# The first two feature-block pairs of w13 as whole blocks, with the sums of x taken meanwhile

## The chip, the cores and the metric

The kernel runs on one core of one Trainium2 chip. Five engines work side by side, each in its own order: TensorE (PE in the rows; PEld is its weight load), VectorE (DVE), ScalarE (ACT), GpSimd (POOL) and SyncE (SP), whose queue issues the weight loads. The metric is device time of one execution in microseconds. The kernel before took 2494.87 us, the median of three runs (2494.54 to 2494.98).

## The reference, cut to what matters

The program is a two-layer encoder with 512 tokens and a model width of 1024. Each layer has a SwiGLU feed-forward block, three token mixers side by side, and a second feed-forward block. The change touches only the first product of the feed-forward blocks, which runs four times (two blocks in each of two layers):

```python
def swiglu(h, w13, w2):
    a, g = jnp.split(h @ w13, 2, axis=-1)
    return (jax.nn.silu(a) * g) @ w2

x = x + 0.5 * swiglu(rms_norm(x, ffn1_norm[l]), ffn1_w13[l], ffn1_w2[l])
```

`w13` has 1024 rows and 2 x 2816 columns: 22 feature blocks of 128 for the value half `a` and 22 for the gate half `g`. All is float32.

## The kernel before

**Layout.** x is kept transposed, as 8 tiles of 128 features by 512 tokens. Each float32 operand of a product is split into a high part in fp32r and a low part (what the high part leaves), and each product is three matmuls: high by high, high by low, low by high. The split of a tile is one cast on ScalarE (the high part) and one subtraction on VectorE (the low part). Weights arrive from SyncE's queue in chunks of 128 x 1024 (`wraw`) and are split in the same way (`whi`, `wlo`, L77 and L78). Raw, split and summed chunks share a pool of 15 slots, so a load waits until a slot is free.

**w13 by seven products instead of eight.** The rms norm's division by the root mean square is put off until after the product, so x only needs its gain. The kernel takes the 8 x tiles in 4 pairs (an even and an odd tile) and cuts the 512 tokens into a left and a right half. For value and gate halves this makes a 2 x 2 by 2 x 2 product, which `wide` (L462) does with seven half-width products instead of eight, at the price of sums on both sides. On the x side, `even` (L413) and `odd` (L424) make the sums `T1` to `T4` from each pair of tiles, and split them. On the weight side, `products` (L91) adds chunks (`wsum`, L104) and yields split chunks in order, three ahead of their use. The 22 feature blocks of each half go in 11 groups, `d` = 0 to 10, of two value blocks and their two gate blocks. One product is a call of `step` (L451): 24 matmuls of 256 columns. So one group is 7 x 24 = 168 matmuls and a stage 11 x 168 = 1848. Four chunks are loaded for each group, four `wsum` are made, and seven chunks are split.

The products of a group share PSUM banks: `11`, `T2`, `T3` and `T4` go one after another into one bank, which ScalarE copies out in between (`copy`, L490); `21` has a bank of its own; `T1` and `22` share a third. The next `T` product into a bank can't start before the copy is out. `gated` multiplies by the norm (`R`) and takes the Silu.

**The norm.** GpSimd squares each x tile and adds it up (`square_sum`, L322): 16 operations, the last of which ends after the last x tile is there. TensorE then transposes the sum (`st`), VectorE reduces it, GpSimd takes the power (`r`), TensorE spreads it (`pr`), ScalarE copies it out as `R` (L350).

**Order.** The tile framework's scheduler sets the order on each engine from its own cost estimates when the program is built; in the first feed-forward block the x side's instructions on ScalarE, VectorE and GpSimd are kept in the order in which the code has them (`manual_schedule`). Each engine takes its instructions strictly in that order. In the first feed-forward block of layer 0 the x tiles come by DMA; in the other three stages they come from the stage before (`pw`, the mixer's output product, or `po`, the product with w2), tile by tile, and VectorE adds each to x (L1049 or L562).

**After w13.** `ffn` (L546) splits the 22 products (`a`, L309) and multiplies by w2 with `mm3` (L218 to L220, 512 columns): the first four output tiles with the feature blocks as the outer loop, so the first matmuls need the first `a`.

Of the kernel before, what the change touches and what calls it, by code (L numbers as in the profile page):

```python
# [12 lines left out]
ALU = mybir.AluOpType  # L13
# [26 lines left out]
class Stream:  # L40
# [23 lines left out]
    def _split(self, upto):  # L64
        while self.ready < min(upto, self.k.nch) and not self.summed(self.ready):
            c = self.ready
            self.load(c + self.k.AHEAD)
            self.split[c] = self.parts(self.raw.pop(c))
            self.ready += 1
# [21 lines left out]
    def products(self, l, name, n):  # L91
# [15 lines left out]
        def start(d):  # L107
            h = held[d] = {"11": raw(d, 0, 0)}
            return self.parts(h["11"], self.cuts(self.pos // CH - 1))

        yield start(0)
        yield start(1)
        for d in range(n):
# [8 lines left out]
            yield self.parts(h["12"])  # L122
# [3 lines left out]
            if 0 < d < n - 1:  # L126
# [27 lines left out]
class Kernel:  # L154
# [95 lines left out]
    def group_rstd(self, pss, srcs, xs, at=(4, 6)):  # L250

        res = g = None
        for k, _ in enumerate(self.group(pss, srcs, xs), 1):
# [159 lines left out]
    def even(self, j, gcol):  # L413

        H = T // 2
        t0, b12 = self.u(name="f0"), self.u(name="fb")
        self.nc.scalar.activation(t0[:, 0:H], self.x[j][:, 0:H], AF.Copy, scale=gcol)
        self.nc.scalar.activation(b12[:, 0:H], self.x[j][:, H:T], AF.Copy, scale=gcol)
        self.nc.vector.tensor_tensor(t0[:, H:T], t0[:, 0:H], b12[:, 0:H], ALU.subtract)
        f0 = self.split(t0, "f0")  # L420
        self.forms.append({"11": [t[:, 0:H] for t in f0], "T1": [t[:, H:T] for t in f0]})
        self.half = t0, b12

    def odd(self, j, gcol):  # L424
# [3 lines left out]
        t0, b12 = self.half  # L428
        f = self.forms[-1]
        t1, t2, t3 = self.u(name="f1"), self.u(name="f2"), self.u(name="f3")  # L430
        nc.scalar.activation(t1, self.x[j], AF.Copy, scale=gcol)
        nc.vector.scalar_tensor_tensor(t2[:, H:T], t0[:, H:T], -1.0, t1[:, H:T], ALU.mult, ALU.subtract)
        nc.vector.tensor_tensor(t2[:, 0:H], t1[:, H:T], b12[:, 0:H], ALU.subtract)
        nc.vector.scalar_tensor_tensor(t3[:, 0:H], t2[:, H:T], -1.0, t1[:, 0:H], ALU.mult, ALU.subtract)
        f1, f2 = self.split(t1, "f1"), self.split(t2, "f2")
        p = j // 2
        if p % 2 == 0:
            self.f3 = self.pair("f3")
        c = slice(p % 2 * H, p % 2 * H + H)
        f3 = self.split_to(t3[:, 0:H], [t[:, c] for t in self.f3])  # L440
        f["21"], f["22"] = [t[:, 0:H] for t in f1], [t[:, H:T] for t in f1]
        f["T3"], f["T2"] = [t[:, 0:H] for t in f2], [t[:, H:T] for t in f2]
        f["T4"] = f3

    def next_form(self, j, gcol):
        (self.odd if j % 2 else self.even)(j, gcol)
        if j == 0:
            self.sqacc = self.u(name="sqacc")
        self.square_sum(self.sqacc, self.x[j], j == 0)
# [12 lines left out]
    def wide(self, l, name):  # L462
# [20 lines left out]
        g = self.rstd(self.sqacc, D, self.att)  # L483
        out, b1, s1 = [], {}, {}
        v = lambda t: t.rearrange("p (e c) -> p e c", e=2)
        state = {}
# [10 lines left out]

        def gated(b, s, half):
            t = self.u(name="t")
            nc.vector.tensor_tensor(t, b, s, ALU.add)  # L500
            nc.vector.tensor_tensor(v(t), v(t), state["R"][:, None, half * H:half * H + H].broadcast_to([P, 2, H]), ALU.mult)
# [3 lines left out]
        start(0)  # L505
        start(1)
        for d in range(n):
            a = [self.u(name="a") for _ in range(2)]
            b2, b3 = self.acc("b"), self.att("b")
            if d == 0:  # L510
                w6, w2, w5 = w(), w(), w()
                for pairs in (range(3), range(3, 4)):
                    self.step(b1[d], w6, "T2", False, pairs)
                    self.step(b2, w2, "21", True, pairs)
# [646 lines left out]
```

## Time and profile before

| what | us |
|---|---|
| median of 3 runs | 2494.87 |
| profiled execution | 2494.28 |
| its span, first to last instruction | 2492.5 |
| w13 of layer 0, first block | to 263.69 from the start of the program |
| w13 of layer 0, second block | 896.87 to 1132.12 |
| w13 of layer 1, first block | 1252.91 to 1485.17 |
| w13 of layer 1, second block | 2118.76 to 2354.00 |

The stages are read from TensorE's rows in order of time: from the first matmul of L459 of a stage to the first matmul into `po`. All other times in this document are us from the start of the span of the profiled execution, unless a row gives ns. "L459" is the matmul of `step`.

### The profile page before, as it was taken

To read this page: it belongs to the slowest core of one execution; us is meant where nothing else is said; L and a number is where in the kernel's file an instruction comes from. 1 tells how busy PE (TensorE), PEld (TensorE's weight loads), DVE (VectorE), ACT (ScalarE), POOL (GpSimd) and SP (SyncE) were. 2 spreads that over 40 slices of the span, in tenths; PEclk is the share of its full clock that TensorE was granted. 3 is DMA by queue.
4 is the path that set the end of the run, shared out by engine and by line. 5 is a ranking of instruction groups with operands and counts; after the bars stand their busy time and mean duration, and the time that the engine had idled before them with its cause. 6 is when DMAs were issued, how large, how long until landed. Compare 5 with 4: busy or idle time off the path is not lost. (4 is left out here: it accounts for less than half of the span.)

```text
span 2492.5 us, 35789 instructions
## 1 busy us (share of the span) xinstructions
PE 2413.5 (97%) x14592; PEld 2146.9 (86%) x14592; DVE 1793.4 (72%) x2575; ACT 1154.5 (46%) x1774; POOL 291.4 (12%) x232
## 2 busy tenths in 40 slices
PE   5999999999999989999999999999999999899997
PEld 4999888888888879998889998888888888899986
DVE  7888655766677698885598884466667777888843
ACT  4444422455555544444255453234655664544520
POOL 3000023100001230000210001230000014100011
PEclk9999999999999999999999999999999999999998
DMA  3333433112121313333223332311221222233331
GB/s 112 102 102 102 127 93 115 51 60 82 63 75 61 119 60 104 109 104 119 92 77 102 104 125 93 112 62 52 76 77 60 68 93 94 77 107 107 120 100 43
DMA packets 62661, 224.22 MB, mean 90 GB/s; under 512 B 7216, under 2 KB 7360, under 8 KB 62496
## 3 DMA queue, kind: packets, MB, share of 16 engines
q1 hardware_dynamic: 61056, 218.19, 27.8%
q8 instruction: 114, 1.87, 0.3%
q0 software_dynamic: 864, 2.70, 0.3%
q10 hardware_dynamic: 576, 1.05, 0.1%
q14 instruction: 51, 0.42, 0.1%
HBM read 219.81 MB, written 2.10 MB: 89 GB/s over the span
## 5 line engine op out<-in xcount | busy, mean ns | idle before, releaser
L78 DVE TENSOR_TENSOR wlo<-wraw,whi 128x1024 fp32r<-128x1024 f32 (+1 forms) x367 | 468.2, 1278 | 227.8 <-PE po L219 135.1
L77 ACT CAST whi<-wraw 128x1024 fp32r<-128x1024 f32 (+1 forms) x367 | 380.2, 1048 | 329.8 <-DVE wlo L78 266.9
L219 PE MATMUL po<-al,whi 128*128 128x512 f32 x704 | 274.7, 390 | 2.8 <-DVE al L309 2.8
L220 PE MATMUL po<-ah,wlo 128*128 128x512 f32 x704 | 274.0, 389 | 0.0
L218 PE MATMUL po<-ah,whi 128*128 128x512 f32 x704 | 270.7, 389 | 0.0
L218 PE MATMUL acc<-hh,whi 128*128 128x512 f32 x672 | 269.9, 402 | 0.0
L220 PE MATMUL acc<-hh,wlo 128*128 128x512 f32 x672 | 263.6, 392 | 0.0
L219 PE MATMUL acc<-hl,whi 128*128 128x512 f32 x672 | 262.9, 391 | 0.0
L78 DVE TENSOR_TENSOR wlo<-wsum,whi 128x1024 fp32r<-128x1024 f32 x176 | 212.3, 1223 | 48.3 <-ACT whi L77 47.0
L77 ACT CAST whi<-wsum 128x1024 fp32r<-128x1024 f32 x176 | 182.1, 1049 | 138.9 <-DVE wsum L104 112.0
L459 PE MATMUL b<-f0h,whi 128*128 128x256 f32 x704 | 203.5, 290 | 39.5 <-ACT f0h L308 39.1
L459 PE MATMUL b<-f0l,whi 128*128 128x256 f32 x704 | 204.1, 290 | 2.2 <-DVE f0l L309 2.2
L459 PE MATMUL b<-f0h,wlo 128*128 128x256 f32 x704 | 203.1, 289 | 0.3 <-DVE wlo L78 0.3
L459 PE MATMUL b<-f1l,whi 128*128 128x256 f32 x704 | 199.6, 283 | 2.3 <-DVE f1l L309 2.3
L459 PE MATMUL b<-f1h,wlo 128*128 128x256 f32 x704 | 199.5, 283 | 0.7 <-DVE wlo L78 0.6
L459 PE MATMUL b<-f2h,whi 128*128 128x256 f32 x704 | 199.8, 284 | 0.2 <-ACT s L490 0.2
L459 PE MATMUL b<-f1h,whi 128*128 128x256 f32 x704 | 199.6, 283 | 0.0
L459 PE MATMUL b<-f2l,whi 128*128 128x256 f32 x704 | 199.2, 283 | 0.0
L459 PE MATMUL b<-f2h,wlo 128*128 128x256 f32 x704 | 199.2, 283 | 0.0
L459 PEld LDWEIGHTS b<-f0h,whi 128*128 128x128 f32 x704 | 138.6, 197 | 41.8 <-ACT f0h L308 41.1
L219 PEld LDWEIGHTS po<-al,whi 128*128 128x128 f32 x704 | 132.1, 188 | 32.9 <-DVE al L309 5.8
L220 PEld LDWEIGHTS po<-ah,wlo 128*128 128x128 f32 x704 | 132.2, 188 | 27.3
(277 smaller groups left out, 5784.6 us busy)
## 6 DMA issues: line engine op xcount, KB each, us to landing
wraw<-in_w SPq DMA_DIRECT2D x409, 512.0 KB, 3.5
x<-in_x SPq DMA_DIRECT2D x8, 256.0 KB, 6.5
rope<-in_rope POOLq DMA_DIRECT2D x6, 256.0 KB, 4.5
out<-o ACTq DMA_DIRECT2D x4, 256.0 KB, 2.8
out<-o SPq DMA_DIRECT2D x4, 256.0 KB, 3.4
dist<-in_cst POOLq DMA_DIRECT2D x1, 448.0 KB, 5.0
wraw<-in_w SPq DMA_DIRECT2D x1, 384.0 KB, 5.0
lv<-in_lam POOLq DMA_DIRECT2D x1, 256.0 KB, 4.2
```

Source lines behind the costliest of these rows:

```text
L77: self.k.nc.scalar.copy(hi[:, part], r[:, part])
L78: self.k.nc.vector.tensor_tensor(lo[:, part], r[:, part], hi[:, part].bitcast(F32), ALU.subtract)
L218: mm(ps, wh, xh, start=start, stop=False)
L219: mm(ps, wh, xl, start=False, stop=False)
L220: mm(ps, wl, xh, start=False, stop=stop)
L459: self.nc.tensor.matmul(ps[:, e * H:e * H + H], w[i][:, c:c + P], x[k], start=first and p == e == n == 0, stop=p == 3 and e == 1 and n == ...
```

## The change

Group 0 of each stage is no longer made with seven products. Its two value blocks and two gate blocks are made as whole blocks into four PSUM banks (`pa`), with the 8 x tiles as the outer loop: 8 tiles x 4 blocks x 3 matmuls = 96 matmuls of 512 columns, from four raw chunks that are split and not summed. It needs each x tile only as gained and split (`plain`), so it begins with tile 0. The sums of x (`sums`) are made from the pairs of tiles meanwhile. `T1` of a pair is written into the right half of the even tile's split form, after the block has read it. The transposes of the norm stand inside the block: `st` behind the fourth tile and `pr` behind the sixth, in the first stage behind the sixth and the eighth. Groups 1 to 10 keep the seven products. Group 1 takes the part that group 0 had: products `11` of groups 1 and 2 come first. In the last group `21` is moved behind `T3`, and the first three `a` are split there.

```diff
-            return self.parts(h["11"], self.cuts(self.pos // CH - 1))
-
-        yield start(0)
+            return self.parts(h["11"])
+
         yield start(1)
-        for d in range(n):
+        yield start(2)
+        for d in range(1, n):
...
-    def group(self, pss, srcs, xs):
-
-        n = len(xs)
+    def group(self, pss, srcs, xs, n, before):
+
         for k in range(n):
             for ps, src in zip(pss, srcs):
+                before(k + (0 if ps is pss[0] else 2))
                 self.mm3(ps, self.w.take(src(k)), xs[k], k == 0, k == n - 1)
             yield
...
+    def plain(self, j, gcol):
+
+        t = self.u(name="f")
+        self.nc.scalar.activation(t, self.x[j], AF.Copy, scale=gcol)
+        self.tiles[j] = t
+        self.h.append(self.split(t, "h"))
         if j == 0:
             self.sqacc = self.u(name="sqacc")
         self.square_sum(self.sqacc, self.x[j], j == 0)
+
+    def sums(self, p):
+
+        H = T // 2
+        nc = self.nc
+        t0, t1 = self.tiles.pop(2 * p), self.tiles.pop(2 * p + 1)
+        if p % 2 == 0:
+            self.f1, self.f3 = self.u(name="f1"), self.pair("f3")
+        c = slice(p % 2 * H, p % 2 * H + H)
+        d, t2, t3 = self.f1[:, c], self.u(name="f2"), self.u(name="f3")
+        nc.vector.tensor_tensor(d, t0[:, 0:H], t0[:, H:T], ALU.subtract)
+        nc.vector.tensor_tensor(t2[:, 0:H], t1[:, H:T], t0[:, H:T], ALU.subtract)
+        nc.vector.scalar_tensor_tensor(t2[:, H:T], d, -1.0, t1[:, H:T], ALU.mult, ALU.subtract)
+        nc.vector.scalar_tensor_tensor(t3[:, 0:H], t2[:, H:T], -1.0, t1[:, 0:H], ALU.mult, ALU.subtract)
+        f2 = self.split(t2, "f2")
+        f3 = self.split_to(t3[:, 0:H], [t[:, c] for t in self.f3])
...
+        pss = [b("pa") for b in (self.acc, self.acc, self.att, self.att)]
+        src = lambda c: lambda k: (name, l, k, [(c, P)])
+        srcs = [src(o + e * P) for e in range(2) for o in (0, FF)]
+        if self.h:
+            _, R = self.group_rstd(pss, srcs, self.h)
+        else:
+            todo = [lambda j=j: self.plain(j, self.g(l, G_FFN1, j)) for j in range(NT)]
+
+            def before(k):
+                while len(self.h) < min(k + 1, NT):
+                    todo.pop(0)()
+
+            with self.tc.manual_schedule(engines={nc.scalar.engine, nc.vector.engine, nc.gpsimd.engine}):
+                _, R = self.group_rstd(pss, srcs, self.h, (6, 8), before)
+                for p in range(4):
+                    self.sums(p)
+        self.h = []
+        for f, t in zip(self.forms, self.diffs):
+            self.split_to(t, f["T1"])
+        self.diffs = []
...
+        for pa, pg in (pss[0:2], pss[2:4]):
+            t, a = self.u(name="t"), self.u(name="a")
+            nc.vector.tensor_tensor(t, pa, R, ALU.mult)
+            self.lookup(t, t, AF.Silu)
+            nc.vector.scalar_tensor_tensor(a, pg, -1.0, t, ALU.mult, ALU.mult)
+            out.append(a)
         start(1)
-        for d in range(n):
+        start(2)
+        for d in range(1, n):
+            last = d == n - 1
...
+            self.step(b1[d], w(), "T2", False)
+            s2 = copy(b1[d])
+            if last:
+                self.a = [self.split(t, "a") for t in out[0:3]]
             else:
-                self.step(b1[d], w(), "T2", False)
-                s2 = copy(b1[d])
                 self.step(b2, w(), "21", True)
-            t1 = gated(b2, s1.pop(d), 0)
-            if d:
-                self.step(b3, w(), "T1", True)
-                self.step(b1[d], w(), "T3", False)
+                t1 = gated(b2, s1.pop(d), 0)
+            self.step(b3, w(), "T1", True)
+            self.step(b1[d], w(), "T3", False)
             s3 = copy(b1[d])
+            if last:
+                self.step(b2, w(), "21", True)
+                t1 = gated(b2, s1.pop(d), 0)
```

Three places of the order as built show what the scheduler makes of it.

The first place is TensorE in the second stage, around the transposes `st` of the norm. In the kernel before (`b1678` is the bank of `T1`, `b1655` that of `T2` and `T3`; `sqacc` is the sum of squares):

```order
L459 MATMUL b1678_8562<-f0h1640_8414,whi1680_8565 128x256
L459 MATMUL b1678_8562<-f0l1641_8415,whi1680_8565 128x256
L459 MATMUL b1678_8562<-f0h1640_8414,wlo1681_8566 128x256
L337 MATMUL st1686_8649<-ident_107,sqacc1587_8220 128x128 x4
L459 MATMUL b1655_8473<-f2h1593_8234,whi1682_8569 128x256
L459 MATMUL b1655_8473<-f2l1594_8235,whi1682_8569 128x256
L459 MATMUL b1655_8473<-f2h1593_8234,wlo1683_8570 128x256
```

And with the change (`pa1641` and `pa1638` are two of the four banks of the whole block; `hh1588` is x tile 3 and `hh1600` x tile 4):

```order
L221 MATMUL pa1641_8369<-hh1588_8156,whi1646_8384 128x512
L222 MATMUL pa1641_8369<-hl1589_8157,whi1646_8384 128x512
L223 MATMUL pa1641_8369<-hh1588_8156,wlo1647_8385 128x512
L340 MATMUL st1651_8436<-ident_107,sqacc1571_8116 128x128 x4
L221 MATMUL pa1638_8366<-hh1600_8209,whi1649_8414 128x512
L222 MATMUL pa1638_8366<-hl1601_8210,whi1649_8414 128x512
L223 MATMUL pa1638_8366<-hh1600_8209,wlo1650_8415 128x512
```

`st` stood behind five products of 24 matmuls of 256 columns; it now stands behind 48 matmuls of 512 columns, between x tiles 3 and 4.

The second place is VectorE in the first stage. In the kernel before, the sums of the first pair of tiles (`f014` to `f3l27`) stand at the start, ahead of the first sums of weights:

```order
L78 TENSOR_TENSOR wlo74_251<-wraw7_93,whi73_250 128x1024
L419 TENSOR_TENSOR f014_111<-f014_111,fb15_112 128x256
L309 TENSOR_TENSOR f0l17_117<-f014_111,f0h16_116 128x512
L432 SCALAR_TENSOR_TENSOR f220_123<-f014_111,f119_122 128x256
L433 TENSOR_TENSOR f220_123<-f119_122,fb15_112 128x256
L434 SCALAR_TENSOR_TENSOR f321_124<-f220_123,f119_122 128x256
L309 TENSOR_TENSOR f1l23_130<-f119_122,f1h22_129 128x512
L104 TENSOR_TENSOR wsum77_258<-wraw10_99,wraw75_254 128x1024
L309 TENSOR_TENSOR f2l25_134<-f220_123,f2h24_133 128x512
L309 TENSOR_TENSOR f3l27_138<-f321_124,f3h26_137 128x256
L104 TENSOR_TENSOR wsum78_260<-wsum77_258,wraw4_86 128x1024
L419 TENSOR_TENSOR f029_144<-f029_144,fb30_145 128x256
```

With the change this is the stretch ahead of the low part of the weights of the first `T1` product (`wlo117`), behind the end of the whole block; `f176`, `f279` and `f283` are sums of x of the third and fourth pairs, and `hl40` and `hl51` the splits of `T1`:

```order
L312 TENSOR_TENSOR hl40_190<-f176_348,hh39_189 128x256
L438 SCALAR_TENSOR_TENSOR f380_352<-f279_351,f45_214 128x256
L104 TENSOR_TENSOR wsum115_484<-wsum101_413,wraw99_409 128x1024
L312 TENSOR_TENSOR f2l82_358<-f279_351,f2h81_357 128x512
L312 TENSOR_TENSOR f3l78_350<-f380_352,f3h77_349 128x256
L435 TENSOR_TENSOR f176_348<-f49_235 128x256
L436 TENSOR_TENSOR f283_363<-f56_262,f49_235 128x256
L437 SCALAR_TENSOR_TENSOR f283_363<-f176_348,f56_262 128x256
L312 TENSOR_TENSOR hl51_238<-f176_348,hh50_237 128x256
L438 SCALAR_TENSOR_TENSOR f384_364<-f283_363,f56_262 128x256
L78 TENSOR_TENSOR wlo117_487<-wsum100_411,whi116_486 128x1024
L312 TENSOR_TENSOR f2l86_370<-f283_363,f2h85_369 128x512
```

The sums of x came first and the weights in between; now all four pairs' sums stand between the whole block and `wlo117`. Ahead of these rows stand a `wsum` that waits for a slot which the last matmuls of the block free, the sums and splits of the first two pairs, and one split of weights.

The third place is TensorE at the end of the first stage, the last rows of each product of the last group. Before (`b403` takes `T2`, `T3` and `T4`, `b421` takes `T1` and `22`; `f2` is the form of `T2` and `T3`, `f3` that of `T4`):

```order
L459 MATMUL b421_2684<-f0h59_215,wlo424_2688 128x256
L459 MATMUL b403_2574<-f2h24_133,whi426_2717 128x256
...
L459 MATMUL b403_2574<-f2h67_233,wlo427_2718 128x256
L459 MATMUL b403_2574<-f3h26_137,whi429_2749 128x256
...
L459 MATMUL b403_2574<-f3h54_203,wlo430_2750 128x256
L459 MATMUL b421_2684<-f1h22_129,whi431_2777 128x256
```

And with the change (`b388` takes `T2`, `T3` and `T4`, `b406` takes `21`, `b407` takes `T1` and `22`):

```order
L459 MATMUL b388_2473<-f2h85_369,wlo409_2587 128x256
L459 MATMUL b406_2584<-hh25_134,whi417_2628 128x256
...
L459 MATMUL b406_2584<-hh57_264,wlo418_2629 128x256
L459 MATMUL b388_2473<-f3h66_322,whi419_2656 128x256
...
L459 MATMUL b388_2473<-f3h77_349,wlo420_2657 128x256
L459 MATMUL b407_2585<-hh25_134,whi422_2686 128x256
```

`T4` followed `T3` into the same bank at once; product `21` now stands between them.

## Rows read from the trace of the kernel before

**Rows 1.** Part 1 of the page: busy us (share of the span) and instructions by engine:
```profile
PE 2413.5 (97%) x14592; PEld 2146.9 (86%) x14592; DVE 1793.4 (72%) x2575; ACT 1154.5 (46%) x1774; POOL 291.4 (12%) x232
```

**Rows 2.** Stretches: length, busy of five engines (instructions), granted clock, DMA share, GB/s:
```profile
58.42:263.69 205.27, 204.59 (x1703) 204.39 (x1703) 173.40 (x205) 101.06 (x124) 0.00 (x0) 1.00 0.34 106
...
926.61:1132.12 205.51, 204.84 (x1705) 204.63 (x1705) 175.22 (x207) 103.36 (x126) 0.00 (x0) 1.00 0.35 108
...
1252.91:1485.17 232.26, 225.68 (x1857) 224.15 (x1855) 200.74 (x233) 116.36 (x143) 8.29 (x5) 0.99 0.32 105
...
2118.76:2354.00 235.24, 225.90 (x1858) 224.75 (x1856) 201.42 (x237) 116.47 (x146) 6.97 (x6) 0.98 0.33 101
```

**Rows 3.** What TensorE waited for, whole program: total us, times, longest us:
```profile
PE b L459 <- ACT f0h L308: 39.1, 7, 12.0
...
PE b L459 <- ACT s L490: 7.0, 8, 1.5
...
PE po L219 <- DVE al L309: 2.8, 4, 1.3
```

**Rows 4.** TensorE in order of time: start, us, group, [idle before <-releaser]:
```profile
14.98 0.80 PE L459 MATMUL b<-f0h,whi 128*128 128x256 f32 x2 [9.71 <-ACT f0h L308]
...
30.32 0.79 PE L459 MATMUL b<-f0h,whi 128*128 128x256 f32 x2 [12.03 <-ACT f0h L308]
...
905.89 0.58 PE L459 MATMUL b<-f0h,whi 128*128 128x256 f32 x1 [6.71 <-ACT f0h L308]
...
1126.26 0.39 PE L459 MATMUL b<-f3h,whi 128*128 128x256 f32 x1 [0.68 <-ACT s L490]
```

**Rows 5.** TensorE in order of time, stretches without idle time before:
```profile
880.09 0.39 PE L219 MATMUL pw<-ml,whi 128*128 128x512 f32 x1
...
896.64 0.39 PE L220 MATMUL pw<-mh,wlo 128*128 128x512 f32 x1
...
908.04 0.42 PE L459 MATMUL b<-f0l,whi 128*128 128x256 f32 x1
...
908.25 0.41 PE L459 MATMUL b<-f0h,wlo 128*128 128x256 f32 x1
...
911.38 0.28 PE L459 MATMUL b<-f0h,wlo 128*128 128x256 f32 x1
```

**Rows 6.** VectorE in order of time, first and second stage:
```profile
10.83 2.05 DVE L78 TENSOR_TENSOR wlo<-wraw,whi 128x1024 fp32r<-128x1024 f32 x1 [1.15 <-ACT whi L77]
...
15.65 1.50 DVE L432 SCALAR_TENSOR_TENSOR f<-f,f 128x256 f32<-128x256 f32 x1
...
38.35 0.42 DVE L433 TENSOR_TENSOR f<-f,fb 128x256 f32<-128x256 f32 x1
...
38.69 0.42 DVE L434 SCALAR_TENSOR_TENSOR f<-f,f 128x256 f32<-128x256 f32 x1
...
39.02 0.68 DVE L309 TENSOR_TENSOR f1l<-f,f1h 128x512 fp32r<-128x512 f32 x1
...
39.62 0.68 DVE L309 TENSOR_TENSOR f2l<-f,f2h 128x512 fp32r<-128x512 f32 x1
...
48.26 1.22 DVE L78 TENSOR_TENSOR wlo<-wraw,whi 128x1024 fp32r<-128x1024 f32 x1
...
49.40 1.22 DVE L78 TENSOR_TENSOR wlo<-wsum,whi 128x1024 fp32r<-128x1024 f32 x1
...
873.27 0.69 DVE L1049 TENSOR_TENSOR x<-x,pw 128x512 f32<-128x512 f32 x1 [2.91 <-PE pw L220]
...
907.10 0.68 DVE L1049 TENSOR_TENSOR x<-x,pw 128x512 f32<-128x512 f32 x1
```

**Rows 7.** GpSimd in order of time, the end of its work on the norm:
```profile
27.20 2.13 POOL L329 TENSOR_TENSOR sqacc<-sqacc,sq 128x512 f32<-128x512 f32 x1
...
909.89 1.34 POOL L329 TENSOR_TENSOR sqacc<-sqacc,sq 128x512 f32<-128x512 f32 x1
...
923.15 1.02 POOL L342 TENSOR_TENSOR r<-ms,mhalf 128x4 f32<-128x4 f32 x1 [11.92 <-DVE ms L340]
```

More of the change, by code (lines that the diff above doesn't have):

```diff
@@ L67, in _split @@
             self.load(c + self.k.AHEAD)
-            self.split[c] = self.parts(self.raw.pop(c))
+            self.split[c] = self.parts(self.raw.pop(c), self.cuts(c))
             self.ready += 1
@@ L240, in finish_gen, with group_rstd @@
                 return e.value
[L242 to L244 removed]
+    def group(self, pss, srcs, xs, n, before):
         for k in range(n):
             for ps, src in zip(pss, srcs):
+                before(k + (0 if ps is pss[0] else 2))
                 self.mm3(ps, self.w.take(src(k)), xs[k], k == 0, k == n - 1)
             yield
[L250 removed]
+    def group_rstd(self, pss, srcs, xs, at=(4, 6), before=lambda k: None):
         res = g = None
[L253 removed]
+        for k, _ in enumerate(self.group(pss, srcs, xs, NT, before), 1):
             if k in at:
@@ L411, in next_h @@
         return h
[L413 to L424, printed above, removed]
-        H = T // 2
-        nc = self.nc
[L428 to L446, printed above, removed]
+    def plain(self, j, gcol):
[3 more added lines that the diff above has]
+        self.h.append(self.split(t, "h"))
         if j == 0:
@@ L449, in next_form @@
         self.square_sum(self.sqacc, self.x[j], j == 0)
+    def sums(self, p):
[12 more added lines that the diff above has]
+        f3 = self.split_to(t3[:, 0:H], [t[:, c] for t in self.f3])
+        h0, h1 = self.h[2 * p:2 * p + 2]
+        left, right = lambda f: [t[:, 0:H] for t in f], lambda f: [t[:, H:T] for t in f]
+        self.forms.append({"11": left(h0), "T1": right(h0), "21": left(h1), "22": right(h1), "T3": left(f2), "T2": right(f2), "T4": f3})
+        self.diffs.append(d)
+    def next_form(self, j, gcol):
+        self.plain(j, gcol)
+        if j % 2:
+            self.sums(j // 2)
     def step(self, ps, w, form, first, pairs=range(4)):
@@ L548, in ffn @@
         self.w.align()
-        if not self.forms:
-            with self.tc.manual_schedule(engines={nc.scalar.engine, nc.vector.engine, nc.gpsimd.engine}):
-                for j in range(NT):
-                    self.next_form(j, self.g(l, G_FFN1, j))
         raw, R = self.wide(l, name + "_w13")
-        a = []
+        a = self.a
         def src(j):
@@ L1052, in mix @@
         pss = [self.att("pw") for _ in range(4)]
-        drain(self.group(pss, [src(j) for j in range(4)], mh))
+        drain(self.group(pss, [src(j) for j in range(4)], mh, NT, lambda k: None))
         for j in range(4):
@@ L1062, in run @@
         self.setup()
-        self.h, self.forms = [], []
+        self.h, self.forms, self.diffs, self.tiles = [], [], [], {}
         for l in range(L):
@@ L1159 @@
 NCH = 410
[L1160 removed]
+SUMS = ((4, 44), (143, 183), (209, 249), (348, 388))
```

27 lines of the change are left out of this document (8 added, 19 removed).

## The prediction, made before the run

> **What bounds the kernel now.** I read part 1 of the page first: TensorE is busy for 97% of the span, VectorE for 72% [rows 1]. So the time is TensorE's work, its pace, and the little that it waits; VectorE matters only where TensorE waits for it. The list of TensorE's waits says where that is: 39.1 us for the first form of x, 7.0 us for ScalarE's copies between products into one bank, 2.8 us for the first `a` [rows 3]. TensorE's order of time then places them. Nearly all of the 39.1 us lies at the starts of the four stages: it first gets a form of x at 14.98, waits another 12.03 us for the second pair's, and in the second stage waits 6.71 us for the last pair's [rows 4]. Behind the starts nothing is lost: from product `T4` of group 0 to the first matmul into `po` stand 10 x 168 + 24 = 1704 matmuls, which took 205.27 and 205.51 us in the first two stages [rows 2], each with one wait of 0.68 us like that at 1126.26 [rows 4].
>
> The pace follows from these stretches: (205.51 - 0.68) / 1704 = 0.1202 us for a matmul of 256 columns. For 512 columns, 880.09 to 896.64 is 73 starts, or 0.2267 us each [rows 5]. After the 6.71 us of waiting, starts are 0.21 us apart, half the pace, until 911.38 [rows 5]: 5.5 us at the lower of the clock's two levels, which costs half of that, 2.7 us, on top of a long wait.
>
> **The change on TensorE without waits.** Out go 168 matmuls per stage, 168 x 0.1202 = 20.2 us; in come 96 of 512 columns, 96 x 0.2267 = 21.8 us: 1.6 us more per stage, 6.3 us in all. A stage without waits then takes 21.8 + 1680 x 0.1202 = 201.9, plus 0.9 us for the two sets of transposes, 224.6 us. The stages now take 263.69 (from the program's start), 235.25, 232.26 and 235.24 us. What can be won is thus some 10.6, 7.7 and 10.6 us in the last three, and more in the first.
>
> The Trainium skill ("TensorE: Matmul & The Clock Gate", section "Back-to-back issue gap") gives N / 2.4 + 2.5 ns as the gap between lone matmuls at the full clock. By that the two shapes take 216 and 109 ns, and the block would cost 96 x 0.216 - 168 x 0.109 = 2.4 us more per stage, an estimate from that page: 3 us more in all than the rows give. The rows have both shapes slower (227 and 120 ns), and theirs are used.
>
> **First stage.** The block needs tile 0 only, so TensorE begins some 8 us earlier. That is not worth 8 us, since something else is late next: `st` stands behind the sixth of eight tiles and needs the last of GpSimd's 16 operations, which ended at 29.33 [rows 7]. That chain is unchanged, and it keeps slowing VectorE: a sum of 256 columns took 1.50 us and a chunk's split 2.05 while GpSimd worked, against 0.42 and 1.22 later [rows 6]. I keep its end. Then come transposes (0.4), the last two tiles (24 x 0.2267 = 5.4), and half of the 2.7 us of clock, since TensorE will have waited but less long: the block ends at about 36.5.
>
> Behind it VectorE is late. The order shows a `wsum` held until the block's last matmuls free its slot, and behind that, up to the low weights of `T1`, 4 operations on chunks, 23 on 256 columns and 3 on 512. From start to start these take 1.14, 0.34 and 0.60 us [rows 6], so 4.6 + 7.8 + 1.8 = 14.2 us, plus 0.3 for ScalarE in between: `T1` goes on at 51.0. TensorE has only `pr` and products `11` of groups 1 and 2 till then, 0.6 + 48 x 0.1202 = 6.4 us, and waits about 8 us, a wait that the kernel before has nowhere after its start. From 51.0 there remain 1680 - 50 = 1630 matmuls, 195.9 us, the clock (2.7), and two waits of 0.9 for copies, because in this order `T3` follows `T2` at once and the next weights are late (1.8). The end is at 251.4 instead of 263.69: 12.3 us.
>
> **Second and fourth stage.** At 896.87 six tiles are ready, so the block starts without the 6.71 us wait. `st` comes after four tiles, 4 x 12 x 0.2267 = 10.9 us later, at 907.8. It needs the last square. x's last addition ran on VectorE at 907.10, 33.8 us after the first at 873.27 [rows 6], and the last square ended at 911.23 [rows 7]. Between these two additions VectorE had 5 operations on chunks, 17 on 512 and 16 on 256 columns; the new order has 5, 17 and 15. So it will be no earlier by its work; it loses some of 2 us of waits for ScalarE. I take 909.7, a wait of 1.9 us. Then `pr`: behind the last addition VectorE has about 6 us of sums and splits before the reduction, then a `wsum` (1.14), and GpSimd's power takes 1.02 [rows 7], which makes `pr` 1.3 us late. With 1.0 for the clock these are 4.2 us, bounded by 0 (VectorE on time) and 9 (the last square at 911.23 as before, `pr` 3 us late, 2.7 of clock). One more wait of 1.0 stands where group 2's first weights sum is late, since its chunk can only load when `T2` of group 1 frees a slot. Sum: 224.6 + 4.2 + 1.0 = 229.8 instead of 235.25: 5.4 us, twice 10.9.
>
> **Third stage.** The same with `po` before it. That product takes 15 us per output tile, so VectorE is less behind, and the last square is due before TensorE reaches `st`. 224.6 + 1.0 = 225.6 instead of 232.26: 6.7 us.
>
> **The end of each stage.** `21` between `T3` and `T4` (2.9 us) covers the copy of `T3`; that wait (0.68 in three stages, more in the third) is in the sums above, since the new ones have none. Three `a` split early remove the 2.8 us before `po` [rows 3]. The three splits cost VectorE 1.8 us that lie beside three products. Against this VectorE and ScalarE lose work: three chunk splits and four weight sums fewer per stage, 8 us of VectorE, and two more operations on 512 columns. VectorE was busy for 173.40 of 205.27 us, or 84%, behind the starts [rows 2], so nothing later is late. Group 0 still loads four chunks, so SyncE's queue has as many loads as before.
>
> **Sum.** 12.3 + 10.9 + 6.7 + 2.8 = 32.7 us. The profiled execution took 2494.28, which becomes 2461.6; the median lies 0.59 above it, so 2462.
>
> **Rivals.**
> *Fewer waits.* If VectorE, which now has no weight sums at the starts, is on time in the later stages, these give 10.6 + 7.7 + 10.6 less three waits of 1.0, or 25.9, and the first stage saves half of its 8 us wait and its clock, 17 in all: with 2.8 that is 46 us, 2449. For it: VectorE had idle time for ScalarE at the starts. Against: the count of its operations is the same.
> *More waits.* The order was made from the scheduler's own estimates, which had VectorE on time where the trace has it 10 us late (the addition for the last tile at 907.10, its product done at 897). If `st` and `pr` take the whole 9 us in the second and fourth stage and the first stage's `T1` is 4 us later: 8 + 2 x 0.6 + 6.7 + 2.8 = 19 us, 2476.
> *Slower: sums of x late behind the block in all four stages.* The 8 us wait before `T1` with its clock (10.7) would come in each. In the later stages VectorE has some 7 us of work between the block and `T1`'s weights and TensorE 11.6, so this decides from a lag of 5 us at the block's end and takes the whole gain at about 15 us. Priced: 12.3 + (5.4 - 10.7) x 2 + (6.7 - 10.7) + 2.8 = 0.5 us gained; with the first stage's lag doubled too, 10 us lost, 2504. Against it: in those stages the order has all four pairs' sums ahead of the reduction for `pr`, so inside the block.
> *The block gains nothing, since the start's waits only move:* 2490 to 2495, the same as the one before without the doubled lag.
>
> **How the numbers follow.** Forecast 0.56, fewer waits 0.17, more waits 0.17, no gain 0.05, slower 0.05. The range is 2446 to 2480: it holds the forecast and both neighbours with their bounds. 0.2% is 5 us, about what a measurement of this kernel can tell from no change. Faster by more: 0.56 + 0.34 + 0.02 of the no-gain cases = 0.92; within it 0.04; slower 0.04.
>
> **What would show it.** In the profile after: 96 matmuls into `pa` at 0.227 us; no wait of over 5 us at the start of the later stages; in the first stage one of 4 to 9 us before the first `st` and one of about 8 us at `T1`, for `wlo`; waits at `st` or `pr` of 1 to 5 us in the second and fourth stage and none in the third; no waits for `al` at the start of `po`. It is wrong if the stretch from group 2 to `po` takes more than 0.1202 us per matmul, if the first stage ends after 257, or if the second stage takes over 234 us.

## The result, and the profile after

The changed kernel takes 2462.19 us (median of 4 runs, 2461.72 to 2463.22), the kernel before 2494.93 beside it (2494.54 to 2496.20): a ratio of 0.9868, 95% interval 0.9851 to 0.9886. The forecast was 2462, with 2446 to 2480 as its range. The total is right; several terms under it are not, and they make up for each other, which is luck. By the profiled executions (span 2460.5 us, before 2492.5):

| us | before | after | gain | forecast |
|---|---|---|---|---|
| first stage, program start to the first `po` | 263.69 | 254.97 | 8.7 | 12.3 |
| second stage | 235.25 | 227.88 | 7.4 | 5.4 |
| third stage | 232.26 | 229.31 | 3.0 | 6.7 |
| fourth stage | 235.24 | 227.89 | 7.4 | 5.4 |
| all the rest (span less the four) | 1526.1 | 1520.5 | 5.6 | 2.8 |
| sum | 2492.5 | 2460.5 | 32.0 | 32.7 |

Part 1 of the page (busy us, share of the span, instructions) answers to [rows 1]:

```profile
PE 2412.6 (98%) x14304; PEld 2134.2 (87%) x14304; DVE 1767.3 (72%) x2543; ACT 1146.1 (47%) x1750; POOL 295.2 (12%) x232
```

TensorE's busy time is as before: 168 short matmuls per stage went and 96 long ones came. So the gain is waits that are gone. TensorE's waits over the program (line waited for, total us, times, longest) answer to [rows 3]:

```profile
PE st L340 <- POOL sqacc L332: 11.8, 4, 6.5
PE pr L349 <- POOL r L345: 5.2, 7, 2.1
PE b L459 <- DVE wlo L78: 4.6, 5, 3.2
PE b L459 <- ACT whi L77: 4.0, 1, 4.0
...
PE b L459 <- ACT s L488: 1.1, 2, 0.7
```

The 39.1 us for the first form of x are gone, and so are the waits for `al`. What stands there now is the row scale: `st` waits for GpSimd's last square. TensorE in order of time places these (start, us, group, idle before and who ended it); the rows answer to [rows 4]:

```profile
32.00 1.12 PE L340 MATMUL st<-ident,sqacc 128*128 128x128 f32 x4 [6.50 <-POOL sqacc L332]
...
40.41 0.36 PE L459 MATMUL b<-hh,whi 128*128 128x256 f32 x1
...
50.40 0.58 PE L459 MATMUL b<-hh,whi 128*128 128x256 f32 x1 [3.99 <-ACT whi L77]
...
54.36 0.58 PE L459 MATMUL b<-hh,wlo 128*128 128x256 f32 x1 [3.16 <-DVE wlo L78]
...
254.97 0.40 PE L221 MATMUL po<-ah,whi 128*128 128x512 f32 x1
...
899.30 0.66 PE L340 MATMUL st<-ident,sqacc 128*128 128x128 f32 x4 [1.45 <-POOL sqacc L332]
...
906.73 0.65 PE L349 MATMUL pr<-ident,r 128*128 128x128 f32 x4 [1.29 <-POOL r L345]
...
930.52 0.39 PE L459 MATMUL b<-f2h,wlo 128*128 128x256 f32 x1 [0.16 <-DVE wlo L78]
...
1247.84 0.85 PE L340 MATMUL st<-ident,sqacc 128*128 128x128 f32 x4 [2.40 <-POOL sqacc L332]
```

In the first stage the reader sees 6.50 us of waiting inside the block and 3.99 + 3.16 us between the first products `11` and `T1` (the two matmuls at 50.40 need only the high weights). The second stage has the two small waits of the forecast, the third one that the forecast did not have. Behind the third stage's wait the clock was low in this execution. Stretches of the third stage and, last, stages 2 to 4 whole (length, busy of five engines, granted clock, DMA share, GB/s):

```profile
1240.00:1246.00 6.00, 5.44 (x24) 4.16 (x23) 5.27 (x6) 2.11 (x4) 3.69 (x3) 1.00 0.50 175
1246.00:1250.00 4.00, 2.16 (x8) 1.87 (x9) 2.96 (x5) 1.60 (x5) 1.71 (x2) 0.77 0.00 0
1250.00:1254.00 4.00, 4.00 (x15) 3.21 (x15) 4.00 (x8) 0.68 (x2) 0.00 (x0) 0.80 0.00 0
...
886.81:1114.69 227.88, 224.98 (x1786) 220.29 (x1784) 196.51 (x233) 115.13 (x144) 7.45 (x5) 1.00 0.32 104
1234.40:1463.71 229.31, 226.60 (x1785) 221.63 (x1784) 195.39 (x232) 112.58 (x142) 7.93 (x6) 0.99 0.31 101
2095.64:2323.53 227.89, 225.25 (x1785) 220.35 (x1784) 195.73 (x233) 115.18 (x144) 9.82 (x5) 1.00 0.32 104
```

### The profile page after: what moved, and what is told of

It reads as the page before. It is cut to its first block, busy times and chain, and to the rows that moved or that the text cites. A ratio compares the mean times of both kernels' runs of the same rounds, so it can differ in the third digit from the quotient of the medians.

```text
span 2460.5 us, 35260 instructions
## 1 busy us (share of the span) xinstructions
PE 2412.6 (98%) x14304; PEld 2134.2 (87%) x14304; DVE 1767.3 (72%) x2543; ACT 1146.1 (47%) x1750; POOL 295.2 (12%) x232
## 4 chain that ended last, share of the span: by engine, by line
PE 87%; DVE 7%; ACT 2%; POOL 1%; issue 1%; DMA 0%; SPq 0%; DVEq 0%; ACTq 0%; POOLq 0%
PE b L459 32%; PE po L222 6%; PE po L221 6%; PE po L223 6%; PE acc L223 6%; PE acc L221 6%; PE acc L222 6%; PE tp L671 2%; PE pm L221 2%; PE pm L223 2%; PE pm L222 2%; DVE wlo L78 1%; PE cs L911 1%; DVE hl L312 1%; PE cp L222 1%
## 5 line engine op out<-in xcount | busy, mean ns | idle before, releaser
L459 PE MATMUL b<-hh,whi 128*128 128x256 f32 x1280 | 364.2, 285 | 4.0 <-ACT whi L77 4.0
L459 PE MATMUL b<-hh,wlo 128*128 128x256 f32 x1280 | 364.1, 285 | 3.2 <-DVE wlo L78 3.2
L459 PE MATMUL b<-hl,whi 128*128 128x256 f32 x1280 | 364.0, 284 | 0.0
L459 PEld LDWEIGHTS b<-hh,whi 128*128 128x128 f32 x1280 | 247.5, 193 | 4.3 <-ACT whi L77 4.2
L459 PEld LDWEIGHTS b<-hh,wlo 128*128 128x128 f32 x1280 | 247.3, 193 | 3.5 <-DVE wlo L78 3.5
L459 PEld LDWEIGHTS b<-hl,whi 128*128 128x128 f32 x1280 | 247.4, 193 | 0.1
L78 DVE TENSOR_TENSOR wlo<-wsum,whi 128x1024 fp32r<-128x1024 f32 x160 | 192.5, 1221 | 50.0 <-ACT whi L77 46.1
L459 PE MATMUL b<-f2h,whi 128*128 128x256 f32 x640 | 181.6, 284 | 0.7 <-ACT s L488 0.7
L459 PE MATMUL b<-f2l,whi 128*128 128x256 f32 x640 | 181.4, 283 | 0.0
L221 PEld LDWEIGHTS po<-ah,whi 128*128 128x128 f32 x704 | 132.2, 188 | 27.3
```

The costliest lines, as they stand in the source:

```text
L78: self.k.nc.vector.tensor_tensor(lo[:, part], r[:, part], hi[:, part].bitcast(F32), ALU.subtract)
L221: mm(ps, wh, xh, start=start, stop=False)
L459: self.nc.tensor.matmul(ps[:, e * H:e * H + H], w[i][:, c:c + P], x[k], start=first and p == e == n == 0, stop=p == 3 and e == 1 and n == ...
```

## The experiments

Each was timed beside the kernel before. "After" is the changed kernel, 2462.2 us, span 2460.5.

**Which part of the change gives what.** First the last group back in its old order, with the block kept:

```diff
-            if d < n - 1:
-                yield self.parts(h["12"])
+            yield self.parts(h["12"])
...
-            if d == n - 1:
-                yield self.parts(h["12"])
...
-            last = d == n - 1
+            last = False
...
-        a = self.a
+        a = []
```

> The changed kernel with the last group of w13 put back in its old order and the first three splits of `a` back behind it; the block of groups of the first two pairs stays. Theory: the last group's part is worth more than the prediction gave it. The four stretches between one w13 stage and the next (and the tail) were 5.6 us shorter in the changed kernel, and the waits of the last `T3` for the scalar copy `s` were 0.68 us in three stages and 1.45 in one before, 3.5 in all; with it undone these come back, 2462 + 9 = 2471 us. Rival, as the prediction had it: only the `al` waits in front of the w2 products come back, 2.8 us, 2465 us.

Measured: 2478.78 us (2476.38 to 2479.97), ratio to before 0.9930 [0.9916, 0.9945]; profiled span 2474.6. That is 16.6 us above the changed kernel by the medians, 14.1 by the spans (the profiled execution is the fastest of its four), far more than either guess. The end of the third stage shows both waits that come back (TensorE in order of time):

```profile
1466.32 0.39 PE L456 MATMUL b<-f3h,whi 128*128 128x256 f32 x1 [1.56 <-ACT s L485]
...
1472.31 1.20 PE L218 MATMUL po<-ah,whi 128*128 128x512 f32 x4
...
1474.78 0.50 PE L219 MATMUL po<-al,whi 128*128 128x512 f32 x1 [1.28 <-DVE al L309]
```

and its list of waits how often:

```profile
PE b L456 <- ACT s L485: 7.5, 5, 2.0
...
PE po L219 <- DVE al L309: 5.1, 4, 1.3
```

Before the change only the third stage ended like this (1.45 and 1.28 us); the other three had 0.68 and 0.50. Behind the block all four end so: 6.8 us of the 7.5 stand there, and the stretches from `po` on are 6.2 us longer than in the changed kernel. Why the three fell into the longer pattern was not followed up.

Then the same edit of the product order, but with the three `a` still split early:

```diff
-            if d == n - 1:
-                yield self.parts(h["12"])
...
             if last:
                 self.a = [self.split(t, "a") for t in out[0:3]]
-            else:
+            if True:
                 self.step(b2, w(), "21", True)
...
-            if last:
-                self.step(b2, w(), "21", True)
-                t1 = gated(b2, s1.pop(d), 0)
```

> The changed kernel with the last group's products in their old order, but the splits of the first three `a` tiles still issued early. Theory: the early splits carry the 5.6 us at the starts of w2, the order of the products the 3.5 us of waits for the copy `s`; so 2462 + 3.5 = 2465.7 us, and the stretches outside w13 stay as short as in the changed kernel. Rival: without the moved product the splits stand on VectorE in front of what the last group's gate needs, and a new wait eats what they save: 2468 to 2471 us.

Measured: 2463.51 us (2462.18 to 2464.71), ratio 0.9870 [0.9853, 0.9886], 1.3 above the changed kernel. The splits alone carry nearly all of it, the waits for `s` at the stage ends too, which the theory had given to the order of the products: with `a` ready, the first `po` matmuls are placed ahead of the last 48 of the stage, and these cover the copy as `21` does. So the early split is what matters, and the order written into the code isn't needed beside it. The new order without the early splits was not run.

And the last group's part alone, on the kernel before (the same three edits of the change, without the block):

```diff
+                if last:
+                    self.a = [self.split(t, "a") for t in out[0:3]]
+                else:
+                    self.step(b2, w(), "21", True)
...
+            if last:
+                self.step(b2, w(), "21", True)
+                t1 = gated(b2, s1.pop(d), 0)
```

> The kernel before with only the last group's new order and its early splits, the first pairs made as before. Theory: the two parts of the change add up, so this takes off what putting it back costs: 6 to 9 us, 2486 to 2489 us, all of it between the last group and the first w2 products of the four stages. Rival: the prediction's 2.8 us, 2492 us.

Measured: 2486.04 us (2484.34 to 2486.66), ratio 0.9960 [0.9945, 0.9974]: 9.4 us, 8.3 by the spans. The four stages give 3.0 of the 8.3 (the waits for `s`), the stretches from `po` on 5.3. So the two parts don't add up: block alone 16.6, last group alone 9.4, both 32.7, all against the kernel before of the same runs.

**Is it VectorE's lighter load?**

```diff
             nc.vector.tensor_tensor(c22, b3, s3, ALU.add)
+            more = self.u(name="more")
+            nc.vector.tensor_tensor(more, R, s3, ALU.add)
```

> The changed kernel with one more addition of 128x512 on VectorE in each of the last ten groups of each w13 stage (its result is not used): 40 of 0.68 us, 27 us in all, about the 26 us by which VectorE's busy time fell. Theory: VectorE's load in the middle of the stages is off the path, and the gain comes from the waits at their starts and ends; 2462 us, within 1. Rival: the gain of 32 us comes from VectorE being freer by 26; putting the same load back costs as much, up to 2494 us.

Measured: 2461.46 us (2461.06 to 2462.07), ratio 0.9862 [0.9848, 0.9877]. VectorE is busy for 1787.4 us instead of 1767.3, less added than I had reckoned but three quarters of what the change had removed, and it costs nothing. The rival is out for the load in groups 1 to 10; that VectorE is freer at the starts and ends of the stages was not tested by this.

**The waits for the row scale in stages 2 to 4.**

```diff
-            _, R = self.group_rstd(pss, srcs, self.h)
+            _, R = self.group_rstd(pss, srcs, self.h, (5, 8))
```

> The changed kernel with the two steps of the row scale (`st`, then `pr`) placed after the fifth and the eighth x tile of the block in stages 2 to 4, instead of after the fourth and the sixth; the first stage is left as it is. Theory: what stages 2 to 4 lose in the block are the waits for `st` and `pr`, 1.45 + 1.29, 2.40 and 1.45 + 0.67 us, and in stage 3 some 1.6 us of low clock that follow its wait: 8.9 us in all, 2453 us. Rival: with `pr` behind the block the four results wait longer for their scale, their banks come free late, and TensorE waits there instead: 2462 to 2470 us. On the clock: if the low clock of stage 3 does not come from the wait of 2.40 us, it stays at 0.77 to 0.80 behind the fourth tile when the wait is gone.

Measured: 2454.32 us (2452.01 to 2455.26), ratio 0.9834 [0.9818, 0.9851], 7.9 below the changed kernel. The third stage whole, and the stretch where `st` stands now:

```profile
1232.28:1457.52 225.24, 225.01 (x1785) 220.40 (x1784) 195.91 (x232) 112.38 (x142) 8.89 (x6) 1.00 0.32 103
...
1244.00:1248.00 4.00, 4.00 (x21) 3.28 (x21) 3.08 (x5) 1.61 (x4) 1.62 (x2) 1.00 0.02 4
```

The third stage is 4.1 us shorter: the wait of 2.40, and what followed it in the changed kernel's execution at the low clock. With the wait gone the clock stays at 1.00. But the low clock does not follow the wait each time. In the run with more work on VectorE the same wait left the clock at 1.00, and `pr`, which TensorE then reached sooner, waited for GpSimd's power instead (TensorE in order of time, then a stretch):

```profile
1248.19 0.66 PE L340 MATMUL st<-ident,sqacc 128*128 128x128 f32 x4 [2.40 <-POOL sqacc L332]
...
1255.61 0.65 PE L349 MATMUL pr<-ident,r 128*128 128x128 f32 x4 [1.28 <-POOL r L345]
```

```profile
1248.00:1252.00 4.00, 3.81 (x19) 3.23 (x20) 3.74 (x8) 1.60 (x4) 0.14 (x1) 1.00 0.00 0
```

Its third stage took 228.95 us, 0.4 less than the changed kernel's, so against that one, too, the third stage with the two steps moved is 3.7 us shorter, by two waits and no clock. The second and fourth stage are shorter by 1.4 and 2.0 us only (226.48 and 225.85). A new wait for the high weights of group 2 stands in them, 0.85 and 0.84 us, and in the second a wait of 0.58 for a copy; the theory had left these out. The late scale costs nothing else; the rival is out.

**The first stage: GpSimd's squares or VectorE's sums?** `st` behind the block:

```diff
-                _, R = self.group_rstd(pss, srcs, self.h, (6, 8), before)
+                for _ in self.group(pss, srcs, self.h, NT, before):
+                    pass
+                rest = self.rstd(self.sqacc, D, self.att)
+                next(rest)
...
+        if rest:
+            start(1)
+            _, R = self.finish_gen(rest)
...
```

> The changed kernel with `st` of the first stage behind the whole block instead of behind its sixth tile, and `pr` behind the first group's first product; VectorE's sums stay behind `st`. Theory: the wait of 6.50 us for GpSimd's last square goes, and VectorE's 14 us of sums move forward with the block's end, since the third sum of weights waits for a slot that the block's last products free; so the first stage ends 6.5 to 9 us earlier, 2453 to 2456 us. Rival: the sums of x on VectorE are the bound of the first stage whatever the block does, `T1` goes on where it did (54.4 us into the span), and the time stays at 2462 us.

Measured: 2455.50 us (2453.69 to 2457.58), ratio 0.9840 [0.9825, 0.9855], 6.7 less than the changed kernel, all in the first stage, which ends at 248.46. TensorE there:

```profile
32.09 0.66 PE L340 MATMUL st<-ident,sqacc 128*128 128x128 f32 x4 [0.34 <-POOL sqacc L332]
...
40.06 1.11 PE L349 MATMUL pr<-ident,r 128*128 128x128 f32 x4 [4.43 <-POOL r L345]
...
49.14 0.57 PE L459 MATMUL b<-hh,wlo 128*128 128x256 f32 x1 [2.79 <-DVE wlo L78]
```

`T1` goes on at 49.14 instead of 54.36, though `pr` now waits 4.43 us for GpSimd's power. The rival falls in its strict form, but part of it holds: the block ends 8.5 us earlier, and VectorE's chain, which ends with the low weights of `T1`, moves by 5.2 only. Its third sum of weights starts at 36.76 instead of 40.03, with no wait for the slot any more:

```profile
36.76 1.22 DVE L104 TENSOR_TENSOR wsum<-wraw,wraw 128x1024 f32<-128x1024 f32 x1
```

That is 3.3 of the 5.2 us. The rest comes from the order as built: three pairs' sums stand ahead of those low weights here, and four in the changed kernel.

With seven of the eight squares left out (`self.seen` is false until the first stage is done):

```diff
-        self.square_sum(self.sqacc, self.x[j], j == 0)
+        if j == 0 or self.seen:
+            self.square_sum(self.sqacc, self.x[j], j == 0)
...
```

> The changed kernel without the squares of x tiles 1 to 7 in the first stage (its row scale there is made from tile 0 alone); GpSimd is idle there. Theory: GpSimd's chain of squares is what `st` waits for, so the wait of 6.50 us goes; and the splits of h on VectorE, 1.6 us each while GpSimd works, fall to 0.7. The block ends at 32 to 34 us instead of 40.2, the sums of x follow it, and the kernel takes 2453 to 2456 us. Rival: `st` waits for something else, or VectorE's sums are the bound and `T1` goes on at 54.4 us as before: 2462 us.

Measured: 2451.19 us (2450.21 to 2452.08), ratio 0.9822 [0.9808, 0.9837], 11.0 less. Without GpSimd beside it VectorE's splits take 0.69 us, and the block ends at 29.2. TensorE and VectorE there:

```profile
39.51 0.58 PE L460 MATMUL b<-hh,whi 128*128 128x256 f32 x1 [4.11 <-ACT whi L77]
...
43.47 0.58 PE L460 MATMUL b<-hh,wlo 128*128 128x256 f32 x1 [3.16 <-DVE wlo L78]
```

```profile
12.22 0.69 DVE L312 TENSOR_TENSOR hl<-f,hh 128x512 fp32r<-128x512 f32 x1
...
29.14 1.22 DVE L104 TENSOR_TENSOR wsum<-wraw,wraw 128x1024 f32<-128x1024 f32 x1
```

Compare with the changed kernel, VectorE in order of time:

```profile
14.60 3.24 DVE L312 TENSOR_TENSOR hl<-f,hh 128x512 fp32r<-128x512 f32 x2
...
33.15 0.69 DVE L342 TENSOR_REDUCE ms<-st 128x4 f32<-128x512 f32 x1 [2.33 <-PE st L340]
...
40.03 1.23 DVE L104 TENSOR_TENSOR wsum<-wraw,wraw 128x1024 f32<-128x1024 f32 x1 [1.39 <-PE pa L222]
...
53.09 1.22 DVE L78 TENSOR_TENSOR wlo<-wsum,whi 128x1024 fp32r<-128x1024 f32 x1
```

The waits before `T1` are the same (4.11 + 3.16 against 3.99 + 3.16), and the whole chain (third sum of weights, sums of x, `T1`) stands 10.9 us earlier. The block ends 11.0 us earlier, but that alone is not why: this run takes away two things at once. The third sum of weights starts at 29.14 without a wait, since VectorE is through with the block's low parts at 22.5 instead of 30.8. In the changed kernel it waits 2.33 us for `st` and 1.39 for the slot that the block's last matmuls free, as the prediction had read it from the order; without these two waits it would start 3.7 us earlier, near the 36.76 of the run before. The other 7.6 us are nearly all VectorE's own work, which is slower beside GpSimd. So GpSimd holds the chain in two ways, by `st` and the block, and by VectorE's pace, and the second is the larger.

**Both moves together** (`st` late in the first stage, and (5, 8) in the others):

> Both moves together: `st` of the first stage behind the block, and `st` and `pr` after the fifth and the eighth tile in stages 2 to 4. Theory: the two gains are in different stages and add up, 6.5 to 9 and 8.9 us: 2444 to 2447 us. Rival: one of them is eaten by late scales, and it is no better than the better of the two alone, 2453 us or more.

Measured: 2447.37 us (2446.41 to 2448.59), ratio 0.9808 [0.9793, 0.9822]: 14.8 less than the changed kernel; 7.9 and 6.7 add up.

**What is left in the first stage.** Three versions on top of that. The sums of x ahead of the row scale:

```diff
-                rest = self.rstd(self.sqacc, D, self.att)
-                next(rest)
                 for p in range(4):
                     self.sums(p)
+                rest = self.rstd(self.sqacc, D, self.att)
+                next(rest)
```

> As the kernel with both moves (2447.4 us), but VectorE makes the sums of x in the first stage before it reduces `st`, so that they don't stand behind the sum of weights that waits for a slot. The squares stay on GpSimd. Theory, that VectorE's slow instructions beside GpSimd are what is left there: VectorE is busy nearly without a gap from 9 us on, so another order of the same work moves little, TensorE waits for the sums where it had waited for `T1`, 2444 to 2450 us. Rival, that the order (the sum of weights waiting for a slot, 36.8 us into the span) holds the sums back: they start at 29 us instead of 38.7, and the first stage ends up to 7 us earlier, 2440 us.

Measured: 2448.20 us (2447.15 to 2449.39), ratio 0.9811 [0.9798, 0.9824], no gain. The sums do start at 29.45, and VectorE works on without a gap. TensorE then waits 6.83 us before `T2`, for a copy that ScalarE has behind its casts of the last sums, and 2.56 for `pr`, whose reduction now stands behind the sums. Time and waits are those of the load theory; the early start that the rival asked for came and gained nothing. Then the squares on ScalarE (in the first stage `plain` makes none any more):

```diff
+    def act_square(self, j, eng):
+        t = self.u(name="sq")
+        self.nc.scalar.activation(t, self.x[j], AF.Square)
+        if j == 0:
+            self.sqacc = t
+        else:
+            eng.tensor_tensor(self.sqacc, self.sqacc, t, ALU.add)
...
+                for j in range(NT):
+                    self.act_square(j, nc.gpsimd)
                 for p in range(4):
                     self.sums(p)
```

> As the kernel with the sums first, but the eight squares of the first stage on ScalarE, after its last cast of the block, and only their seven additions on GpSimd. Theory: in the run without seven of the squares VectorE's splits took 0.69 and 1.23 us instead of 1.6 and 2.06, and the block ended at 29.2 us; with the squares off GpSimd until the block's splits are done the same holds here, the sums follow from 22 us on, TensorE reaches `T2` at about 37 us and waits little: 2436 to 2441 us. Rival: GpSimd's additions now fall beside the sums and slow them as they had slowed the splits, and the scale R comes late: 2443 to 2447 us.

Measured: 2447.31 us (2447.00 to 2447.94), ratio 0.9807 [0.9794, 0.9821]. The rival holds, 0.3 us above its range: the block ends at 29.0, but `st` behind it waits 3.21 us for GpSimd's seven additions, which end at 32.2 and now run beside the sums. VectorE there, during and after:

```profile
23.03 1.51 DVE L448 TENSOR_TENSOR f<-f,f 128x256 f32<-128x256 f32 x1
...
33.31 0.41 DVE L448 TENSOR_TENSOR f<-f,f 128x256 f32<-128x256 f32 x1
```

Last, the additions on VectorE:

```diff
-                for j in range(NT):
-                    self.act_square(j, nc.gpsimd)
                 for p in range(4):
                     self.sums(p)
+                for j in range(NT):
+                    self.act_square(j, nc.vector)
```

> As the last one, but the seven additions of squares on VectorE, behind its sums of x; GpSimd makes only the power of R in the first stage. Theory: nothing slows VectorE's sums (0.42 us each), they end by 37 us; seven additions of 0.6 us then hold R back to about 46 us, which the products `T2` and `T1` cover in part: 2436 to 2441 us, near the one with the additions on GpSimd. Rival: the late R keeps the block's banks full, and TensorE waits for the first bank for some 5 us: 2444 us or more.

Measured: 2444.88 us (2443.24 to 2445.56), ratio 0.9797 [0.9783, 0.9810], the fastest of all: 17.3 us below the changed kernel and 50 below the one before. The sums end at 37, as expected, but the time is the rival's, 3.9 us above the theory's range:

```profile
40.14 0.58 PE L471 MATMUL b<-f2h,whi 128*128 128x256 f32 x1 [4.94 <-ACT s L500]
...
45.00 1.11 PE L340 MATMUL st<-ident,sq 128*128 128x128 f32 x4 [1.51 <-DVE sq L436]
...
50.13 1.12 PE L349 MATMUL pr<-ident,r 128*128 128x128 f32 x4 [1.88 <-POOL r L345]
```

`T2` goes into the bank of `11` and needs ScalarE's copy of it first, and that copy now stands behind the squares; `st` and `pr` come late behind the additions. These three waits, and not the block's banks as the rival had it, are what the squares and the late R cost.

## Why the prediction was right, and which terms were not

**TensorE without waits.** Right: 224.6 us was worked out for a stage without waits, and the third stage without its wait took 225.24. In the changed kernel, stage 2 is 224.6 + 1.45 + 1.29 + 0.16 and 0.4 more.

**First stage, 12.3 us, measured 8.7: mis-sized, mainly in one number.** The steps came as forecast: `st` waits for the last square, a sum of weights waits for a slot that the block's end frees, 14.2 us of VectorE's work follow (from 40.03 to 54.3 in the trace), `T1` waits (7.15, forecast about 8), and from `T1` to `po` it is 200.6 us where 200.4 was worked out. What failed was "That chain is unchanged" and "I keep its end": the last of GpSimd's operations on the norm (15 in the trace, not 16) ended at 31.94, not at 29.33 [rows 7]:

```profile
29.82 2.12 POOL L332 TENSOR_TENSOR sqacc<-sqacc,sq 128x512 f32<-128x512 f32 x1
```

The stretch to 32 us before, and after:

```profile
3.00:32.00 29.00, 6.96 (x23) 5.07 (x22) 22.60 (x17) 9.07 (x15) 21.99 (x15) 1.00 0.50 179
```

```profile
3.00:32.00 29.00, 20.30 (x79) 14.40 (x77) 24.26 (x15) 15.83 (x23) 25.00 (x15) 0.96 0.64 233
```

GpSimd's 15 operations are the same and took 25.0 us instead of 22.0, beside a VectorE that was busy for 24.3 instead of 22.6. So the slowing works both ways here, and a chain that slows its neighbour is not a fixed point. With the clock behind the wait (24 products in 7.3 us instead of 5.4) the block ended at 40.2 instead of 36.5, and `T1` went on 3.4 us later. The forecast also had the block's end as the only bound of VectorE's chain; by the runs above VectorE's own work was late by nearly as much.

**Second and fourth stage, 5.4 each, measured 7.4.** The waits for `st` (1.9 forecast, 1.45) and `pr` (1.3; 1.29 and 0.67) were sized well from a count of VectorE's operations. The two terms that had no row, 1.0 for the clock and 1.0 for group 2's weights, came out at 0 and 0.16.

**Third stage, 6.7, measured 3.0: the step failed.** "VectorE is less behind, and the last square is due before TensorE reaches `st`" is wrong. VectorE's order of time:

```profile
1243.65 0.68 DVE L578 TENSOR_TENSOR d<-po,R 128x512 f32<-128x512 f32 x1
...
1244.59 0.68 DVE L579 SCALAR_TENSOR_TENSOR x<-d,x 128x512 f32<-128x512 f32 x1
```

The last `po` was done at 1234.6; its result was read 9 us later, behind the sums of the pair before. That is about as late as in the second stage, where the last `pw` was done at 887.0 and its result read at 895.13. VectorE has hardly a gap in these 9 us: what stands in front is work queued between two tiles (a split of weights, sums, splits), which the time that a tile takes on TensorE doesn't shorten. The wait cost 2.40 us, and the low clock behind it 1.6 more in this execution; where the clock held, `pr` waited 1.28 instead.

**The last group, 2.8 us and the waits for `s` in the stage sums (3.5), 6.3 together: mis-sized.** Put on the kernel before, it gave 8.3 by the spans; taken from the changed kernel, 14.1. That leaves 26.4 of the forecast's 32.7 us for the block, which alone gave 16.6. The list of waits undercounts. The start of `po` in the kernel before, TensorE in order of time:

```profile
263.69 1.09 PE L218 MATMUL po<-ah,whi 128*128 128x512 f32 x4
265.28 0.50 PE L219 MATMUL po<-al,whi 128*128 128x512 f32 x1 [0.50 <-DVE al L309]
...
267.23 1.07 PE L218 MATMUL po<-ah,whi 128*128 128x512 f32 x4
...
270.24 0.39 PE L218 MATMUL po<-ah,whi 128*128 128x512 f32 x1
```

The first 12 products took 3.54 us and the next 12 took 3.01, where the changed kernel takes 2.74 for 12: the wait listed as 0.50 is 1.07 in these 24 products, since the idle column leaves out the time in which the last product still runs, and a short second wait is not listed at all. And with the block alone all four stages end with the longer waits, so that much of what the table books as the block's is due to the early splits. Why the block lengthens them stays open.

**The rivals.** "Slower", sums late behind the block in every stage, did not come: in stages 2 to 4 no wait of over 0.4 us follows the block. "No gain" is out. The second and fourth stage came out between the forecast and "fewer waits" (7.4, with 5.4 and 9.6 forecast). The first stage came out at 8.7, near the 8 of "more waits", and of the rivals only "slower" priced the third stage under 6.7. The terms missed by -3.6, +1.9, -3.7, +1.9 and +2.8 us; that they add up to -0.7 is luck, and the forecast owes its place to it.

## What to carry to other kernels

When a wait is removed at the start of a stage, ask for the next operand in line that nothing on TensorE covers; here it was a row scale that is only needed behind the block, and moving its two small steps one and two tiles later was worth a quarter of the whole change. Take the parts of a change off one at a time: two parts that give 16.6 and 9.4 us alone gave 32.7 together, and the smaller-looking one, three splits issued early, carried up to half of it (16.6 of 32.7 when taken from the changed kernel). Do not keep the end of a chain on GpSimd as it was when VectorE's work beside it becomes denser.

## What the runs showed of the hardware

VectorE and GpSimd slow each other. A split of 512 columns took 0.69 us with GpSimd idle and 1.6 beside its squares; a sum of 256 columns 0.41 and 1.51. A square on GpSimd took 1.04 us beside an idle VectorE and 1.48 to 2.02 beside a busy one (GpSimd in order of time, without seven of the squares and in the changed kernel):

```profile
3.96 1.04 POOL L328 TENSOR_TENSOR sqacc<-x 128x512 f32<-128x512 f32 x1 [1.97 <-DMA x<-in_x]
```

```profile
13.56 2.02 POOL L331 TENSOR_TENSOR sq<-x 128x512 f32<-128x512 f32 x1
```

The split and the sum on VectorE take their own time plus 0.9 and 1.1 us, near that of one square on GpSimd. The Trainium skill ("SBUF — State Buffer", section "SBUF: two separate sides") says that a VectorE operation with two SBUF inputs and a GpSimd operation that reads SBUF share a port pair by an exclusive lock, held for a whole instruction. The 0.9 and 1.1 us agree with that; no trace here shows the lock itself.

The clock: behind 2.40 us of idle time in the third stage the granted clock was 0.77 and 0.80 in the next two stretches of 4 us of the changed kernel. It fell behind the same wait in two experiments as well, with the first stage's `st` late and without seven of its squares (0.68 and 0.73 in the 4 us around `st`), and stayed at 1.00 in three others: with the last group's old order, with the early splits only, and with more on VectorE. So the same idle time lowers the clock in one execution and not in another. Behind 1.45 us in the second and fourth stage it stayed at 1.00.
